# Placing TensorE's operands in SBUF at multiples of 2 KB, with the mixing outputs at staggered offsets

## The chip, the core and the metric

The kernel runs on one core of a Trainium2 chip. The metric is the time of one execution in device microseconds, as the median of several runs. All times below are microseconds unless they are marked ns. Offsets in SBUF are bytes from the start of a partition, the same on all 128 partitions.

## The reference

Two layers act on 256 positions of width 2048. Each layer is a mixing block and a feed-forward block, each with a residual and a layer norm behind it. The mixing block of layer 0 is a gated MLP plus a multiscale pool; that of layer 1 is a gated linear recurrence by chunks. All of them reduce to large products `h = x @ w`, and everything is float32.

```python
x:  [256, 2048]
layer 0:  h = x @ ev_w_in   # 2048 x 3072
          mix = concat(spatial_gating(h), multiscale_pool(h)) @ ev_w_out   # 2048 x 2048
layer 1:  h = x @ od_w_in   # 2048 x 8192
          mix = (rms_norm(hgrn2(h)) * sigmoid(g)) @ od_w_out               # 2048 x 2048
x = layer_norm(ALPHA * x + mix)
# in both layers
hc = conv3(x @ w_up)        # 2048 x 11264
x = layer_norm(ALPHA * x + (silu(hc[:, :5632]) * hc[:, 5632:]) @ w_down)   # 5632 x 2048
```

## The kernel before

**Products.** Weights come from HBM in tiles `w` of 128 x 4 x 512 floats (1 MB), through a ring of three. Each is split into two float32r tiles, `wh` (its rounded value, written by ScalarE at L144) and `wl` (the rest, written by VectorE at L147), in rings of three. The activations, transposed, are split in the same way into `xh` and `xl`. A product is then three matmuls for each of the four slices of 128 rows: `xh*wh`, `xh*wl`, `xl*wh` (L291, L359, L513). The activation slice of 128 columns (512 B a partition) is the stationary operand, which a weight load (PEld in the profile) puts into the array ahead of each matmul. The weight slice of 512 columns (2 KB a partition) is the moving one.

**Who uses which tiles.** `chunk` (L291) runs the mixing layers' input products on `xh`, `xl`, their output products on `yh`, `yl` (names `YT` in the code), and the first columns of a feed-forward block. `strassen` (L359) runs the rest of the up products on `xh`, `xl` and on combined tiles `sh`, `sl`; `down` and `last_down` (L513) run the down products on another `yh`, `yl`, which belong to the feed-forward block (`GT` in the code). So the name `y` stands for two sets of tiles: at L291 for the mixing outputs, at L513 for the feed-forward's.

**Order.** Each engine's instructions stand in the order in which the code issues them. Small work (transposes, gates, convolutions) is put between matmuls by `later` and `tick`.

**Where tiles lie.** Tile pools hand out SBUF in the order in which they are opened, one tile behind the other. The built program puts the operands of TensorE's large products here (offset, and what is left of it by 2048 and by 256):

| tiles | before | by 2048 | by 256 |
|---|---|---|---|
| `xh`, `xl` (8 tiles of 4 KB) | from 34464 | 1696 | 160 |
| `sh`, `sl` (2 of 8 KB) | from 67232 | 1696 | 160 |
| `wh`, `wl` (6 of 8 KB) | from 109600 | 1056 | 32 |
| mixing `yh`, `yl` (8 of 4 KB) | from 158752 | 1056 | 32 |
| feed-forward `yh`, `yl` (4 of 4 KB) | from 176544 | 416 | 160 |

A stationary slice begins a multiple of 512 B behind its tile's start, a moving slice a multiple of 2048 B.

Of the kernel before, what the change touches and what calls it, by code (L numbers as in the profile page):

```python
# [9 lines left out]
F32 = mybir.dt.float32  # L10
F32R = mybir.dt.float32r
# [7 lines left out]
P = 128  # L19
S = 256  # L20
D = 2048
DFF = 5632
NF = DFF // P
# [3 lines left out]
SKEW = 3  # L27
UNIT = ("P1", "s", "P2", "s", "P3", "o", "P7", "o", "P6", "o", "P5", "o", "P4", "s", "s")
BUFS = 3


class Weights:
# [78 lines left out]
    def room(self, kind):  # L111
# [6 lines left out]
        ring = self.ring.get(tag, [])  # L118
        n = 1 if kind else BUFS
        return len(ring) < n or ring[-n]["last"] < self.n_cast  # L120
# [46 lines left out]
def block_kernel(ctx: ExitStack, tc: tile.TileContext, a, out):  # L167
    nc = tc.nc
    V, A, G, T = nc.vector, nc.scalar, nc.gpsimd, nc.tensor

    const = ctx.enter_context(tc.tile_pool(name="const", bufs=1))
    resid = ctx.enter_context(tc.tile_pool(name="resid", bufs=1))
    acts = ctx.enter_context(tc.tile_pool(name="acts", bufs=1))
    gbp = ctx.enter_context(tc.tile_pool(name="gbp", bufs=1))
    small = ctx.enter_context(tc.tile_pool(name="small", bufs=2))
    raw = {0: ctx.enter_context(tc.tile_pool(name="raw", bufs=BUFS))}
    hl = ctx.enter_context(tc.tile_pool(name="hl", bufs=3))
    dram = ctx.enter_context(tc.tile_pool(name="dram", bufs=1, space=bass.MemoryType.DRAM))
# [32 lines left out]
    plan_ffn(1)  # L211


    cst = const.tile([P, 3, P], F32, name="cst")
    ident, tri, aft = (cst[:, i] for i in range(3))
    mhalf = const.tile([P, 4], F32, name="mhalf")
# [3 lines left out]
    def new_T(kind, g, pool=acts):  # L220
        h = pool.tile([P, 4, S], F32R, name=f"{kind}h{g}", tag=f"{kind}h{g}")
        l = pool.tile([P, 4, S], F32R, name=f"{kind}l{g}", tag=f"{kind}l{g}")
        return h, l

    def split(dst, src, hs, scale=None):

        h, l = dst[0][hs], dst[1][hs]
        if scale is None:
            A.activation(h, src, AF.Copy)
            V.tensor_tensor(out=l, in0=src, in1=h.bitcast(F32), op=ALU.subtract)  # L230
        else:
            A.activation(h, src, AF.Copy, scale=scale)
            V.scalar_tensor_tensor(out=l, in0=src, scalar=scale, in1=h.bitcast(F32),
                                   op0=ALU.mult, op1=ALU.subtract)

    XT = [new_T("x", g) for g in range(4)]
    with tc.tile_pool(name="xload", bufs=2) as xl:

# [25 lines left out]
    def later(n, fn):  # L264
        waiting.append([n, fn])
# [173 lines left out]
    def transpose(dst, src):  # L439
        T.transpose(dst, src, ident)  # L440
# [20 lines left out]
    def transpose_split(dst, src, t):  # L461

        pt = aux.tile([P, 4, P], F32, name="pt", tag="aux")
        for k in range(4):
            transpose(pt[:, k], src[:, k * P:(k + 1) * P])
        split(dst, pt, np.s_[:, :, t * P:(t + 1) * P])
# [8 lines left out]
    def out_proj(Ts_by_chunk, n, scale_first, g_ap=None, b_ap=None, order=None, final=False):  # L475

        last = g_ap is not None
        if last:
            gt, bt = load_gb(g_ap, b_ap)
            sts = [small.tile([P, 4, 6], F32, name=f"st{t}") for t in range(2)]  # L480
            new = [new_T("x", g) for g in range(4)] if not final else None
# [42 lines left out]
    def down(c, Ts, scale):  # L524

        w = W.take()
        for t in range(2):
            ps = aux.tile([P, 512], F32, name="pd", tag="aux")
            product(ps, w, Ts, t)
            tick(0.5)  # L530
            add_x(t, c, ps, scale)

    def last_down(Ts, g_ap, b_ap, final):

        gt, bt = load_gb(g_ap, b_ap)
        sts = [small.tile([P, 4, 6], F32, name=f"st{t}") for t in range(2)]
        new = [new_T("x", g) for g in range(4)] if not final else None
        pool_of = {}

# [62 lines left out]

    ymix = ExitStack()
    yp = ymix.enter_context(tc.tile_pool(name="ymix0", bufs=1))
    YT = [new_T("y", g, yp) for g in range(4)]
    with tc.tile_pool(name="work0", bufs=1) as wk:
        v_t = [wk.tile([P, 1024], F32, name=f"v{t}") for t in range(2)]
        b_t = [wk.tile([P, 1024], F32, name=f"xb{t}") for t in range(2)]
# [44 lines left out]
        def pool(gi):  # L653
# [13 lines left out]
            for d in range(2):  # L667
                kb = (gi % 2) * 2 + d
                split(YT[2 + gi // 2], py[:, d], np.s_[:, kb, :], scale=psc[:, gi * 2 + d:gi * 2 + d + 1])

        def after_u(c):
            def f(t, ps):
                u = wk.tile([P, 512], F32, name="u", bufs=2)
                A.activation(u, ps, AF.Gelu_apprx_tanh)
                V.tensor_tensor(out=u, in0=u, in1=v_t[t][:, c * 512:(c + 1) * 512], op=ALU.mult)
                later(1, lambda: transpose_split(YT[c], u, t))
            return f
# [14 lines left out]
        chunk(XT, 4, after_u(1))  # L692
        XT = out_proj([YT[g] for g in (2, 3, 0, 1)], 4, True, a["ln1_g"][0], a["ln1_b"][0])
    ymix.close()


    def ffn(l, XT, final):
        with ExitStack() as pools:
            wk = pools.enter_context(tc.tile_pool(name=f"workf{l}", bufs=1))
            raw[1] = pools.enter_context(tc.tile_pool(name=f"rawq{l}", bufs=1))  # L700
            W.open += 1
            cw = wk.tile([P, 4, 2 * NF], F32, name="cw")
            G.dma_start(cw, a["conv"][l].rearrange("p (j n) -> p j n", j=4))

            def h_tile(name="h", tag=None):
                return wk.tile([P, 512], F32, name=name, tag=tag or "h", bufs=1 if tag else 4)

            GT = {}

            def post(p, part, hs, hc):  # L710

                o = wk.tile([P, 4, S], F32, name="hc", tag="hc", bufs=2)
                hc[part] = o
                if part == 1:
                    GT[p] = tuple(wk.tile([P, 4, S], F32R, name=f"y{i}", tag=f"y{i}", bufs=2) for i in "hl")
                for kk in range(2):
                    pt = aux.tile([P, 2, S], F32, name="ph", tag="aux")
                    for k in range(2):
                        for tt in range(2):
                            fs = slice((2 * kk + k) * P, (2 * kk + k + 1) * P)  # L720
                            transpose(pt[:, k, tt * P:(tt + 1) * P], hs[tt][:, fs])
                    two = np.s_[:, 2 * kk:2 * kk + 2]
                    for k in range(2):
                        blk = part * NF + p * 4 + 2 * kk + k
                        ob = o[:, 2 * kk + k]
                        A.activation(ob, pt[:, k], AF.Identity, scale=cw[:, 2, blk:blk + 1],  # L726
                                     bias=cw[:, 3, blk:blk + 1])
                        for s, w in ((2, 0), (1, 1)):
                            V.scalar_tensor_tensor(  # L729
                                out=ob[:, s:S], in0=pt[:, k, 0:S - s], scalar=cw[:, w, blk:blk + 1],  # L730
                                in1=ob[:, s:S], op0=ALU.mult, op1=ALU.add)
                    if part == 0:
                        A.activation(o[two], o[two], AF.Silu)
                    else:
                        V.tensor_tensor(out=o[two], in0=o[two], in1=hc[0][two], op=ALU.mult)
                        split(GT[p], o[two], two)

            def ready(p):
                hc = {}
                return lambda part, hs: later(0.5 if part and p == 10 else 1, lambda: post(p, part, hs, hc))  # L740

            def conv(part, done):
                hs = [h_tile() for _ in range(2)]

                def f(t, ps):
                    A.activation(hs[t], ps, AF.Copy)
                    if t == 1:
                        done(part, hs)
                return f

            done = ready(0)
            chunk(XT, 4, conv(0, done), head=True)
            XS = combine(XT, lambda: wk.tile([P, 4, S], F32, name="cmb", tag="hc", bufs=2))
            chunk(XT, 4, conv(1, done))
            for p in range(1, 11):
                downs = [lambda c=c, p=p: down(c, GT[p - 1], p == 1) for c in range(4)]
                strassen(XT, XS, h_tile, ready(p), downs[:4 if p < 10 else 2])
            for fn in downs[2:]:
                fn()
            XT = last_down(GT[10], a["ln2_g"][l], a["ln2_b"][l], final)  # L760
            del raw[1]
        return XT

    XT = ffn(0, XT, False)


    yp = ymix.enter_context(tc.tile_pool(name="ymix1", bufs=1))
    YT = [new_T("y", g, yp) for g in range(4)]
    with tc.tile_pool(name="work1", bufs=1) as wk:
        lb = gbp.tile([P, D], F32, name="lb", tag="g")  # L770
        omlb = gbp.tile([P, D], F32, name="omlb", tag="b")
# [15 lines left out]
        def heads4(hg):  # L787
# [111 lines left out]
            def after_g(t, ps):  # L899
                g = wk.tile([P, 512], F32, name="gg", tag="tb", bufs=2)  # L900
                A.activation(g, ps, AF.Sigmoid)
                V.tensor_tensor(out=o_s[t], in0=o_s[t], in1=g, op=ALU.mult)
                later(1, lambda: transpose_split(YT[hg], o_s[t], t))

# [5 lines left out]
        for hg in range(4):  # L910
            heads4(hg)
        XT = out_proj(YT, 4, True, a["ln1_g"][1], a["ln1_b"][1])
    ymix.close()

    ffn(1, XT, True)


# [74 lines left out]
```

## Time and profile before

| | us |
|---|---|
| median of 3 runs (lowest to highest) | 2256.62 (2254.83 to 2259.21) |
| the profiled execution's own time | 2258.18 |
| span of its trace | 2256.5 |
| TensorE matmuls (PE) busy | 2215.6, 9971 instructions |
| weight loads (PEld) busy | 1803.7 |
| VectorE (DVE) busy | 1672.4 |
| ScalarE (ACT) busy | 1165.1 |
| GpSimd (POOL) busy | 103.4 |
| DMA | 466.98 MB, mean 207 GB/s |

Matmuls overlap in the profile: one takes some 0.39 from its start to its modelled end, while the next starts some 0.23 behind it. How fast TensorE works is therefore read from the distance between starts (called a step below), not from busy time.

### The profile page before, as it was taken

How to read it: one execution, taken by the hardware profiler on the slowest of the kernel's cores; microseconds unless marked ns; L12 is line 12 of the kernel's file. 1: busy time of each engine (PE TensorE's matmuls, PEld its weight loads, DVE VectorE, ACT ScalarE, POOL GpSimd, SP SyncE). 2: the span in 40 equal slices, each digit the busy share in tenths (PEclk: the TensorE clock that was granted, in tenths of full speed). 3: DMA queues.
4: the chain of work that ended last, by engine and by line, in shares of the span. 5: the costliest groups of instructions: out<-in, count | busy, mean ns of one | idle time of the engine just before them, and what ended most of it. 6: DMA issues, size and time to landing. Idle time of an engine off the chain costs nothing. (4 is left out here: it accounts for less than half of the span.)

```text
span 2256.5 us, 24752 instructions
## 1 busy us (share of the span) xinstructions
PE 2215.6 (98%) x9971; PEld 1803.7 (80%) x9971; DVE 1672.4 (74%) x1604; ACT 1165.1 (52%) x1088; POOL 103.4 (5%) x116
## 2 busy tenths in 40 slices
PE   9999999999999999979999999999999999999997
PEld 7888788888888888868888888878888888888885
DVE  5545878888888888876455555578788888888887
ACT  5443455555555555535354554336555555555552
POOL 1000200000000000020000000020000000000000
PEclk9999999999999999989999999999999999999999
DMA  8647456767766676535444454845777667677742
GB/s 316 261 161 277 159 179 218 230 224 242 218 213 220 214 235 224 187 126 193 158 167 173 167 210 168 279 153 168 226 241 242 202 211 221 216 232 243 239 149 116
DMA packets 68595, 466.98 MB, mean 207 GB/s; under 512 B 8080, under 2 KB 8736, under 8 KB 13312
## 3 DMA queue, kind: packets, MB, share of 16 engines
q1 hardware_dynamic: 60656, 411.56, 50.0%
q0 software_dynamic: 7824, 53.84, 11.5%
q8 instruction: 78, 1.28, 0.2%
q14 instruction: 37, 0.30, 0.0%
HBM read 421.32 MB, written 2.11 MB: 188 GB/s over the span
## 5 line engine op out<-in xcount | busy, mean ns | idle before, releaser
L147 DVE TENSOR_TENSOR wl<-w,wh 128x2048 fp32r<-128x2048 f32 (+1 forms) x450 | 1004.3, 2234 | 463.8 <-ACT wh L144 463.6
L144 ACT ACTIVATE wh<-w 128x2048 fp32r<-128x2048 f32 (+1 forms) x474 | 854.1, 1807 | 726.2 <-PE pd L513 260.5
L359 PE MATMUL ps<-wh,xh 128*128 128x512 f32 x880 | 350.5, 398 | 0.0
L359 PE MATMUL ps<-wh,xl 128*128 128x512 f32 x880 | 347.4, 395 | 0.0
L359 PE MATMUL ps<-wl,xh 128*128 128x512 f32 x880 | 347.0, 394 | 0.0
L291 PE MATMUL ps<-wh,xh 128*128 128x512 f32 x832 | 334.4, 403 | 1.2 <-ACT wh L144 1.2
L291 PE MATMUL ps<-wl,xh 128*128 128x512 f32 x832 | 330.1, 397 | 0.6 <-DVE wl L147 0.5
L291 PE MATMUL ps<-wh,xl 128*128 128x512 f32 x832 | 329.2, 396 | 0.0
L513 PE MATMUL pd<-wh,yh 128*128 128x512 f32 x664 | 263.0, 396 | 0.0
L513 PE MATMUL pd<-wl,yh 128*128 128x512 f32 x664 | 262.6, 395 | 0.0
L513 PE MATMUL pd<-wh,yl 128*128 128x512 f32 x664 | 261.9, 395 | 0.0
L359 PEld LDWEIGHTS ps<-wh,xl 128*128 128x128 f32 x880 | 165.7, 188 | 38.8
L359 PEld LDWEIGHTS ps<-wl,xh 128*128 128x128 f32 x880 | 165.9, 189 | 36.9
L359 PEld LDWEIGHTS ps<-wh,xh 128*128 128x128 f32 x880 | 165.8, 188 | 37.0
L291 PEld LDWEIGHTS ps<-wh,xh 128*128 128x128 f32 x832 | 157.7, 190 | 37.5 <-ACT wh L144 2.6
L291 PEld LDWEIGHTS ps<-wl,xh 128*128 128x128 f32 x832 | 157.7, 190 | 36.7 <-DVE wl L147 2.4
L291 PEld LDWEIGHTS ps<-wh,xl 128*128 128x128 f32 x832 | 157.3, 189 | 36.4
L513 PEld LDWEIGHTS pd<-wh,yl 128*128 128x128 f32 x664 | 125.4, 189 | 29.4
L513 PEld LDWEIGHTS pd<-wh,yh 128*128 128x128 f32 x664 | 125.5, 189 | 29.2
L513 PEld LDWEIGHTS pd<-wl,yh 128*128 128x128 f32 x664 | 125.4, 189 | 29.3
L729 DVE SCALAR_TENSOR_TENSOR hc<-ph,cw,hc 128x254 f32<-128x254 f32 (+1 forms) x352 | 145.7, 476 | 1.0 <-ACT hc L726 1.0
L359 PE MATMUL ps<-wh,sh 128*128 128x512 f32 x320 | 126.3, 395 | 0.5 <-ACT u L371 0.5
(191 smaller groups left out, 2284.3 us busy)
## 6 DMA issues: line engine op xcount, KB each, us to landing
w<-in_w_up SPq DMA_DIRECT2D x176, 1024.0 KB, 4.9
w<-in_w_down SPq DMA_DIRECT2D x88, 1024.0 KB, 4.9
w<-in_w_od_in SPq DMA_DIRECT2D x64, 1024.0 KB, 4.8
w<-w POOLq DMA_DIRECT2D x40, 1024.0 KB, 8.0
w<-in_w_ev_in SPq DMA_DIRECT2D x20, 1024.0 KB, 5.5
w<-in_w_ev_out SPq DMA_DIRECT2D x16, 1024.0 KB, 4.9
w<-in_w_od_out SPq DMA_DIRECT2D x16, 1024.0 KB, 5.8
w<-in_w_ev_in SPq DMA_DIRECT2D x16, 256.0 KB, 6.1
```

The lines of the kernel that those rows point to most:

```text
L144: self.nc.scalar.activation(h[:, sl], w[:, sl], AF.Copy)
L147: eng.tensor_tensor(out=l[:, sl], in0=w[:, sl], in1=h[:, sl].bitcast(F32), op=ALU.subtract)
L291: T.matmul(ps[t], s[:, k, ts], m[:, k], start=(gi == 0 and k == 0 and i == 0), stop=(gi == n - 1 and k == 3 and i == 2))
L359: T.matmul(bank_, x[:, k, ts], m[:, k], start=(id(bank_) not in started), stop=(end and k == 3 and i == 2), skip_group_check=True)
L513: T.matmul(ps, x[:, k, t * P:(t + 1) * P], m[:, k], start=(k == 0 and i == 0), stop=(k == 3 and i == 2))
L729: V.scalar_tensor_tensor(out=ob[:, s:S], in0=pt[:, k, 0:S - s], scalar=cw[:, w, blk:blk + 1], in1=ob[:, s:S], op0=ALU.mult, op1=ALU.add)
```

## The change

The pool `small` is opened ahead of the large pools instead of behind them, and a tile `edge` of 976 B fills up to 20480, so that all that follows, up to the weights' tiles, begins at multiples of 2048. The tile `cw` (the convolution's coefficients, 1408 B) gets a pool of its own behind the feed-forward's, so that it no longer stands ahead of their tiles. The mixing outputs, which would then also begin at multiples of 2048, are spread by pads of 32 to 64 B (once 224 B): a different offset for each of the eight tiles.

```diff
+EDGE = 244
+STAGGER = ((0, 32, 64, 96, 128, 160, 192, 256), (0, 224, 288, 320, 352, 384, 416, 448))
...
     const = ctx.enter_context(tc.tile_pool(name="const", bufs=1))
+    small = ctx.enter_context(tc.tile_pool(name="small", bufs=2))
+    edge = ctx.enter_context(tc.tile_pool(name="edge", bufs=1))
     resid = ctx.enter_context(tc.tile_pool(name="resid", bufs=1))
     acts = ctx.enter_context(tc.tile_pool(name="acts", bufs=1))
     gbp = ctx.enter_context(tc.tile_pool(name="gbp", bufs=1))
-    small = ctx.enter_context(tc.tile_pool(name="small", bufs=2))
...
+    edge.tile([P, EDGE], F32, name="edge")
...
+    def staggered(pool, at):
+        tiles, end = [], 0
+        for i in range(8):
+            if at[i] > end:
+                pool.tile([P, (at[i] - end) // 4], F32, name=f"pad{i}")
+                end = at[i]
+            tiles.append(pool.tile([P, 4, S], F32R, name=f"y{'hl'[i % 2]}{i // 2}"))
+        return [(tiles[2 * g], tiles[2 * g + 1]) for g in range(4)]
...
-    YT = [new_T("y", g, yp) for g in range(4)]
+    YT = staggered(yp, STAGGER[0])
...
-            cw = wk.tile([P, 4, 2 * NF], F32, name="cw")
+            cwp = pools.enter_context(tc.tile_pool(name=f"cw{l}", bufs=1))
+            cw = cwp.tile([P, 4, 2 * NF], F32, name="cw")
...
-    YT = [new_T("y", g, yp) for g in range(4)]
+    YT = staggered(yp, STAGGER[1])
```

In the changed program the places are these:

| tiles | by 2048 | by 256 |
|---|---|---|
| `xh`, `xl`, `sh`, `sl`, `wh`, `wl`, feed-forward `yh`, `yl` | 0 | 0 |
| mixing `yh0`, `yl0`, ... `yl3`, layer 0 | 0, 32, 64, 96, 128, 160, 192, 256 | 0, 32, 64, 96, 128, 160, 192, 0 |
| mixing `yh0`, `yl0`, ... `yl3`, layer 1 | 0, 224, 288, 320, 352, 384, 416, 448 | 0, 224, 32, 64, 96, 128, 160, 192 |

The order of the instructions is the same on PE, DVE, ACT and SP. On POOL two rows move. First, how POOL stands around the end of the output product of layer 0 before the change (`cw` the convolution's coefficients, `w_0<-w_2` the first accumulating DMA between weight tiles, `rs` a layer norm's scale, `wl` weight splits done by POOL):

```order
L655 DMA wp<-in_w_pool 128x2x256 x2
L75 DMA w_0_1787<-w_2_1791 128x2048
L448 TENSOR_TENSOR rs<-rs,mhalf 128x1
L147 TENSOR_TENSOR wl_1592<-w_40_1523,wh_1591 128x512 x4
L147 TENSOR_TENSOR wl_1604<-w_41_1559,wh_1603 128x512 x4
L703 DMA cw<-in_conv 128x352
L448 TENSOR_TENSOR rs<-rs,mhalf 128x1
```

And the same place on POOL with the change, with its own line numbers:

```order
L669 DMA wp<-in_w_pool 128x2x256 x2
L718 DMA cw<-in_conv 128x352
L77 DMA w_0_1801<-w_2_1805 128x2048
L462 TENSOR_TENSOR rs<-rs,mhalf 128x1
L149 TENSOR_TENSOR wl_1603<-w_40_1534,wh_1602 128x512 x4
L149 TENSOR_TENSOR wl_1615<-w_41_1570,wh_1614 128x512 x4
L462 TENSOR_TENSOR rs<-rs,mhalf 128x1
```

The load of `cw` is issued one place ahead of the accumulating DMA, since `cw` no longer lies where the mixing outputs lie. The same move is made in layer 1.

## Rows read from the trace of the kernel before

**Rows 1.** The page, parts 1 and 2: busy time, granted clock.

```profile
PE 2215.6 (98%) x9971; PEld 1803.7 (80%) x9971; DVE 1672.4 (74%) x1604; ACT 1165.1 (52%) x1088; POOL 103.4 (5%) x116
...
PEclk9999999999999999989999999999999999999999
```

**Rows 2.** PE's waits on others: us in total, times, longest.

```profile
PE pt L440 <- DVE x L459: 19.1, 9, 4.1
```

**Rows 3.** PE's groups by line and form: busy us, mean ns, idle before.

```profile
L359 PE MATMUL ps<-wh,xh 128*128 128x512 f32 x880 | 350.5, 398 | 0.0
...
L291 PE MATMUL ps<-wh,xh 128*128 128x512 f32 x832 | 334.4, 403 | 1.2 <-ACT wh L144 1.2
...
L513 PE MATMUL pd<-wh,yh 128*128 128x512 f32 x664 | 263.0, 396 | 0.0
...
L359 PE MATMUL ps<-wh,sh 128*128 128x512 f32 x320 | 126.3, 395 | 0.5 <-ACT u L371 0.5
...
L291 PE MATMUL ps<-wh,yh 128*128 128x512 f32 x256 | 100.4, 392 | 0.0
...
L513 PE MATMUL ps<-wh,yh 128*128 128x512 f32 x40 | 16.7, 418 | 5.0 <-ACT yh L229 5.0
```

**Rows 4.** Timeline of PE, mixing output products: start, us, engine, line, instruction.

```profile
166.46 0.40 PE L291 MATMUL ps<-wl,yh 128*128 128x512 f32 x1
...
243.53 0.39 PE L291 MATMUL ps<-wh,yl 128*128 128x512 f32 x1
...
1420.13 0.39 PE L291 MATMUL ps<-wl,yh 128*128 128x512 f32 x1
...
1497.22 0.39 PE L291 MATMUL ps<-wh,yl 128*128 128x512 f32 x1
```

**Rows 5.** Timeline of PE, an input product of layer 1 and feed-forward turns.

```profile
1117.14 0.39 PE L291 MATMUL ps<-wl,xh 128*128 128x512 f32 x1
...
1141.78 0.40 PE L291 MATMUL ps<-wh,xl 128*128 128x512 f32 x1
...
771.65 0.39 PE L359 MATMUL ps<-wl,xh 128*128 128x512 f32 x1
...
837.53 0.39 PE L359 MATMUL ps<-wl,xh 128*128 128x512 f32 x1
...
890.05 0.39 PE L359 MATMUL ps<-wh,xl 128*128 128x512 f32 x1
...
686.36 0.40 PE L359 MATMUL ps<-wh,xh 128*128 128x512 f32 x1
686.61 0.40 PE L359 MATMUL ps<-wl,xh 128*128 128x512 f32 x1
```

**Rows 6.** Windows: length; PE, PEld, DVE, ACT, POOL busy (instructions); clock; DMA share, GB/s.

```profile
166.46:243.54 77.08, 77.08 (x342) 63.81 (x340) 42.28 (x34) 25.93 (x17) 2.08 (x3) 1.00 0.72 257
837.53:890.06 52.53, 52.53 (x228) 42.59 (x227) 44.77 (x39) 27.17 (x21) 0.84 (x1) 1.00 0.80 255
1117.14:1141.79 24.65, 24.65 (x108) 19.98 (x107) 14.82 (x14) 13.69 (x13) 0.00 (x0) 1.00 0.54 190
```

**Rows 7.** ACT's waits in the feed-forward block of layer 0 (310 to 960).

```profile
ACT wh L144 <- PE pd L513: 125.8, 39, 3.7
```

**Rows 8.** Timeline and window of PE in a stretch at the lower clock.

```profile
992.80 0.63 PE L513 MATMUL pd<-wl,yh 128*128 128x512 f32 x1
...
994.50 0.62 PE L513 MATMUL pd<-wh,yl 128*128 128x512 f32 x1
...
992.60:994.80 2.20, 2.20 (x6) 0.50 0.00 0
```

**Rows 9.** Timeline of POOL in layer 0, and ACT's uses of `cw`.

```profile
184.65 0.93 POOL L75 DMA_DIRECT2D w<-w  x1 [62.81 <-DVE st L494]
...
256.02 0.60 POOL L703 DMA_DIRECT2D cw<-in_conv  x1 [0.21 <-issue]
...
L726 ACT ACTIVATE hc<-ph,cw x176: 543/555/572, 288.2 to 2216.4; 128x256 f32<-128x256 f32 x176
```

## The prediction

> **What bounds the kernel now.** I read the page first. TensorE's matmuls are busy for 98% of the span, at the full granted clock in all slices but one [rows 1]. Then the waits of PE: the largest of them, the transposes behind a layer norm, is 19.1 us in 9 times [rows 2]. So the time is the sum of TensorE's own steps, and the other engines wait for it: in the feed-forward block ScalarE waits 125.8 us for a matmul of L513 to give a weight buffer free [rows 7]. A change of the time has to come out of the step from one matmul's start to the next, which no view prints. I took it from the timeline, as first and last start of an unbroken run over the number of steps in it. The groups give the counts: three of each kind, so 3 x (880 + 320 + 832 + 664 + 40) = 8,208 large matmuls on `x`, `s` and the feed-forward's `y`, and 3 x 256 = 768 on the mixing outputs [rows 3].
>
> The two sets don't run at one pace. A mixing output product takes 341 matmuls from 166.46 to 243.53: 77.07 / 340 = 226.7 ns a step; in layer 1 the same 340 steps take 77.09, 226.7 ns again [rows 4]. (The window counts 342, one of which began before it [rows 6].) The input product from 1117.14 to 1141.78 has 107 matmuls: 24.64 / 106 = 232.4 ns; a feed-forward turn from 837.53 to 890.05 has 227: 52.52 / 226 = 232.4 ns [rows 5, 6]. The granted clock is 1.00 in all three stretches [rows 6], which is the 2.4 GHz level. So a step costs 5.7 ns more wherever the stationary tile is not a mixing output.
>
> What differs? Not the code: the input product and the output product are both written by `chunk`, at L291, with the same three matmuls for a slice and the same moving tiles `wh`, `wl`. Not the load: DMA moves 257 GB/s beside the output product, and 190 and 255 beside the other two; VectorE is busy for 42.28 of 77.08 beside the output product, 14.82 of 24.65 beside the input product and 44.77 of 52.53 in the feed-forward [rows 6]. The first two are near each other, and 25 points more of VectorE leave the longer step where it is. What is left is the place. Mixing outputs and weights begin at the same remainder, 1056 by 2048; `xh` and `sh` are 640 ahead of the weights and the feed-forward's `yh` 640 behind. Both are 128 off by 256, and slices move this by multiples of 512 only, so that each product has one relation throughout. That fits one longer step for both, and a shorter one at distance 0.
>
> **The change, part by part.**
>
> *Large tiles to multiples of 2 KB.* All of the 8,208 matmuls get the relation that the output products have now: stationary and moving tile at the same remainder. I take the 226.7 ns step for them. Counted over the trace, 7,952 of them are followed by another large matmul 220 to 245 ns later; the other 256 stand beside transposes, behind waits or at the lower clock, where a step is (994.50 - 992.80) / 4 = 425 ns [rows 8], and are taken to stay. 7,952 x 5.7 ns = **-45.3 us**. Bounds of this term by the same rows: 8,208 x 5.7 = 46.8 if the rest shrinks too; nothing if it isn't the place.
>
> *Do the others follow?* They have to be 2.5% faster in the same stretches. VectorE would go from 44.77 / 52.53 = 85% to 87% in a feed-forward turn [rows 6], and its casts are ahead, since ScalarE's half of them waits for PE's buffers [rows 7]; DMA goes from 255 GB/s at a share of 0.80 to some 261 at 0.82 [rows 6]. So nothing takes over. The stalls at the layer norms stay as they are [rows 2].
>
> *Mixing outputs staggered.* These 768 now run at 226.7 ns, at distance 0. With the change `yh` is stationary twice and `yl` once in every three; weighing the tiles so, 64 + 32 of 384 matmuls of layer 0 and 64 of 384 of layer 1 keep a multiple of 256, and 608 of 768 get another distance. Some 748 of the steps are unbroken, so 608 / 768 x 748 = 592 steps are at stake. The trace has no distance but 0 and 128 for these products. Below: nothing, if 128 alone costs more and the rest as little as 0. Above: all at the longest single step of the feed-forward, 686.61 - 686.36 = 0.25 in rounded starts (241 ns unrounded), 592 x 14.3 = 8.5 us. At 232.4 ns it is 592 x 5.7 = 3.4. I take half of that, **+1.7 us**, as some of the distances should be as good as 0 and some as bad as 128.
>
> *`cw` and `small`.* The order of instructions changes on POOL alone: `cw` is issued one place earlier, ahead of the DMA at 184.65, and no longer at 256.02; its first use is at 288.2 [rows 9]. It was not waited for before and lands earlier now: nothing. It takes its wait from the DMA that stood at 184.65, so the scale of the layer norm behind them is not held up longer than before. If that cover went, the price would be one landing in each layer, some 5 us each.
>
> *Transposes.* Their operands move against each other as well: some 600 short matmuls whose step is about 0.11. The same share of it, 5.7 / 232.4, would be 2.7 ns each, 1.6 us either way. I take nothing.
>
> The sum, on the profiled execution's own time: 2258.2 - 45.3 + 1.7 = 2214.6. That execution was 1.6 over the median of the runs shown, so as a median **2213.0 us**, 1.9% less.
>
> **A rule against it.** The step differs by 5.7 ns between runs of the same instructions at the same clock [rows 4 to 6]. The Trainium skill says the opposite of what I conclude from this: in "TensorE: Matmul & The Clock Gate", section "Step-by-step: what each phase is for", the streamed operand and the weight load have independent read ports, and "Loading the next tile's weights doesn't steal SBUF read bandwidth from the running matmul"; and "SBUF — State Buffer", section "Who interferes with whom", has TensorE never wait on anyone. By that rule the place of a tile is worth nothing and the sum is 2256.6. This trace doesn't agree with the strict form of it, since 226.7 and 232.4 ns stand side by side; but it doesn't show that the place is the reason, and so the rule stays as the first rival.
>
> **The rivals.**
>
> *No change (0.07).* The place is not the reason, and something that I don't see in the rows sets the pace of the two kinds of product: then the 8,208 keep 232.4 ns, the mixing products 226.7, and the time is 2256.6. For it: only two products have the shorter step, both the output products of mixing layers. Against it: the longer step is the same to 0.1 ns at L291 and at L359 with L513, under different loads.
>
> *Slower (0.04).* It is not the distance but the place itself that counts, and a start at 0, which no large operand has before, is worse than either remainder that the trace has (32 and 160 by 256). The place is every feed-forward and input step. At the longest single step of the feed-forward, 241 ns, for all: 7,952 x 8.6 = 68 us, 2325. It decides from 232.4 ns on; at 233 the time is 0.2% above before.
>
> *More than forecast (0.03).* Even the output products are not at the floor: at the lower clock a step is 425 ns [rows 8], and half of that is 213. If a start at a whole 2 KB takes away the rest too, 7,952 x 19 = 151 us more or less all come off: 2106. The Trainium skill's "Back-to-back issue gap" ("TensorE: Matmul & The Clock Gate") would put an undisturbed step of 512 columns at some 216 ns; an estimate by it is 7,952 x 16.4 = 130 us off, 2126. Against this case: 680 steps at distance 0 all keep to 226.7.
>
> *Part of it (0.03).* A start at 0 lies between the two: 229.5 ns, 7,952 x 2.9 = 23 us off, 2234.
>
> **How the numbers follow.** My forecast has 0.83. Its own range: 46.8 off and no stagger gives 2209.8; 45.3 off and 8.5 for the stagger gives 2219.8. With 2 us for the transposes either way and the half spread of the runs, 2.2, this is 2206 to 2224. I give 2205 to 2225; all rivals lie outside it, which leaves out 17 in 100. A measurement of this kernel tells about 0.2% from nothing, 4.5 us. Faster by more than that: forecast, part and more, 0.89. Within it: 0.07. Slower: 0.04.
>
> **What the profile of the changed kernel would show.** Right: a run of large matmuls in the input products and in the feed-forward steps by 226 to 227.5 ns; a turn of the feed-forward, 65.88 from 771.65 to 837.53 before [rows 5], takes 64.3 (276 matmuls x 5.7 ns = 1.6 less); PE's waits for VectorE stay near 19 us and no wait for `wh` or `wl` appears in the feed-forward. The stagger: 77.1 for 340 steps of a mixing output product grows to between 77.1 and 81, and steps change when `chunk` goes on to the next group. Wrong: input and feed-forward steps that stay at 232 (the first rival) or rise; a step below 226; or steps at 226.7 with new gaps in front of matmuls, which would mean that the casts or the weight loads don't follow.

## The result, and the profile after

The changed kernel takes 2220.46 us (median of 4 runs, 2219.09 to 2221.51), the kernel before 2257.91 beside it (4 runs). The ratio is 0.9836, 95% interval 0.9819 to 0.9853: 1.6% faster. The profiled execution took 2219.09, its span 2217.4; against the one shown before that is 39.1 us less.

The page of the changed kernel, parts 1 and 2, to be read beside [rows 1]:

```profile
PE 2175.4 (98%) x9971; PEld 1798.1 (81%) x9971; DVE 1670.8 (75%) x1604; ACT 1161.9 (52%) x1088; POOL 102.8 (5%) x116
...
PEclk9999999999999999989999999999999999999998
```

The busy shares are the same within one point, and the clock in all slices but the last; VectorE and ScalarE have lost 1.6 and 3.2 us of busy time, TensorE 40.2. So TensorE still sets the time, and it got through the same 9971 instructions sooner. The timeline of PE shows where. Changed lines: L305 is L291 of before, L373 is L359, L527 is L513. First the input product and the feed-forward turn that answer to [rows 5]:

```profile
1097.30 0.40 PE L305 MATMUL ps<-wl,xh 128*128 128x512 f32 x1
...
1121.33 0.39 PE L305 MATMUL ps<-wh,xl 128*128 128x512 f32 x1
...
759.42 0.40 PE L373 MATMUL ps<-wl,xh 128*128 128x512 f32 x1
...
823.76 0.40 PE L373 MATMUL ps<-wl,xh 128*128 128x512 f32 x1
...
875.00 0.39 PE L373 MATMUL ps<-wh,xl 128*128 128x512 f32 x1
```

The same 106 steps now take 24.03, 226.7 ns each instead of 232.4. The 226 steps from 823.76 to 875.00 take 51.24, 226.7 ns instead of 232.4. A whole turn, 759.42 to 823.76, takes 64.34 instead of 65.88. The mixing output products, which answer to [rows 4], went the other way:

```profile
164.23 0.40 PE L305 MATMUL ps<-wl,yh 128*128 128x512 f32 x1
...
243.14 0.40 PE L305 MATMUL ps<-wh,yl 128*128 128x512 f32 x1
...
1395.04 0.39 PE L305 MATMUL ps<-wl,yh 128*128 128x512 f32 x1
...
1473.81 0.40 PE L305 MATMUL ps<-wh,yl 128*128 128x512 f32 x1
```

340 steps take 78.91 and 78.77 instead of 77.07 and 77.09: 232.1 and 231.7 ns. The windows over three of these stretches, beside [rows 6] (PE, PEld, DVE, ACT, POOL busy, clock, DMA share, GB/s), show that the load beside TensorE is what it was:

```profile
164.23:243.15 78.92, 78.92 (x342) 63.85 (x340) 42.61 (x34) 25.95 (x17) 2.65 (x4) 1.00 0.71 253
823.76:875.01 51.25, 51.25 (x228) 42.42 (x227) 44.66 (x39) 27.14 (x21) 0.85 (x1) 1.00 0.82 262
1097.30:1121.34 24.04, 24.04 (x108) 19.90 (x107) 14.70 (x14) 13.70 (x13) 0.00 (x0) 1.00 0.54 192
```

The waits of PE (us, times, longest) have hardly moved, as [rows 2] and the idle times of [rows 3] (5.0 at L513, 1.2 for `wh` at L291) say beside these lines; the waits for `wh` fall in the first 100 us, in the input product of layer 0:

```profile
PE pt L454 <- DVE x L473: 18.3, 9, 4.3
PE ps L527 <- ACT yh L243: 5.0, 2, 2.5
PE ps L305 <- ACT wh L146: 2.3, 2, 1.3
```

### The profile page after: what moved, and what is told of

Read it like the earlier page. It is cut to its first block, busy times and chain, and to the rows that moved or that the text cites. A ratio compares the mean times of both kernels' runs of the same rounds, so it can differ in the third digit from the quotient of the medians.

```text
span 2217.4 us, 24753 instructions
## 1 busy us (share of the span) xinstructions
PE 2175.4 (98%) x9971; PEld 1798.1 (81%) x9971; DVE 1670.8 (75%) x1604; ACT 1161.9 (52%) x1088; POOL 102.8 (5%) x116
## 5 line engine op out<-in xcount | busy, mean ns | idle before, releaser
L373 PE MATMUL ps<-wh,xh 128*128 128x512 f32 x880 | 345.8, 393 | 0.0
L373 PE MATMUL ps<-wh,xl 128*128 128x512 f32 x880 | 342.6, 389 | 0.0
L373 PE MATMUL ps<-wl,xh 128*128 128x512 f32 x880 | 342.6, 389 | 0.0
L305 PE MATMUL ps<-wh,xh 128*128 128x512 f32 x832 | 330.3, 398 | 2.3 <-ACT wh L146 2.3
L305 PE MATMUL ps<-wl,xh 128*128 128x512 f32 x832 | 325.8, 392 | 0.3 <-DVE wl L149 0.3
L305 PE MATMUL ps<-wh,xl 128*128 128x512 f32 x832 | 325.0, 391 | 0.0
L527 PE MATMUL pd<-wh,yh 128*128 128x512 f32 x664 | 259.1, 390 | 0.0
L527 PE MATMUL pd<-wl,yh 128*128 128x512 f32 x664 | 258.8, 390 | 0.0
L527 PE MATMUL pd<-wh,yl 128*128 128x512 f32 x664 | 258.4, 390 | 0.0
L373 PEld LDWEIGHTS ps<-wh,xl 128*128 128x128 f32 x880 | 165.2, 188 | 34.4
L373 PEld LDWEIGHTS ps<-wh,xh 128*128 128x128 f32 x880 | 165.3, 188 | 33.0
L373 PEld LDWEIGHTS ps<-wl,xh 128*128 128x128 f32 x880 | 165.3, 188 | 32.9
L305 PEld LDWEIGHTS ps<-wh,xh 128*128 128x128 f32 x832 | 156.9, 189 | 34.9 <-ACT wh L146 3.2
L305 PEld LDWEIGHTS ps<-wl,xh 128*128 128x128 f32 x832 | 156.9, 189 | 32.9 <-DVE wl L149 2.2
L305 PEld LDWEIGHTS ps<-wh,xl 128*128 128x128 f32 x832 | 156.6, 188 | 33.0
L527 PEld LDWEIGHTS pd<-wh,yl 128*128 128x128 f32 x664 | 124.9, 188 | 26.4 <-DVE yl L244 0.4
L527 PEld LDWEIGHTS pd<-wh,yh 128*128 128x128 f32 x664 | 125.0, 188 | 25.9
L527 PEld LDWEIGHTS pd<-wl,yh 128*128 128x128 f32 x664 | 124.9, 188 | 25.8
L373 PE MATMUL ps<-wh,sh 128*128 128x512 f32 x320 | 124.7, 390 | 0.5 <-ACT u L385 0.5
```

Of the source, the lines that this page charges most:

```text
L305: T.matmul(ps[t], s[:, k, ts], m[:, k], start=(gi == 0 and k == 0 and i == 0), stop=(gi == n - 1 and k == 3 and i == 2))
L373: T.matmul(bank_, x[:, k, ts], m[:, k], start=(id(bank_) not in started), stop=(end and k == 3 and i == 2), skip_group_check=True)
L527: T.matmul(ps, x[:, k, t * P:(t + 1) * P], m[:, k], start=(k == 0 and i == 0), stop=(k == 3 and i == 2))
```

## The experiments

Each kernel is named by what it changes. The times are medians beside runs of the kernel before on the same chip; steps are means over a trace's unbroken steps (220 to 245 ns), and where the text gives one without rows, it is counted over all of them. Every kernel below computes the whole reference.

**The changed kernel without the stagger.** Is it the stagger that lengthened the mixing products?

```diff
-STAGGER = ((0, 32, 64, 96, 128, 160, 192, 256), (0, 224, 288, 320, 352, 384, 416, 448))
+STAGGER = ((0,) * 8, (0,) * 8)
```

> The changed kernel without the stagger: the eight mixing outputs begin at multiples of 2048 too. Distance theory (a step is short when the stationary and the moving tile begin at the same remainder by 512): the steps of the two mixing output products go from 231.9 ns back to 226.7, 750 x 5.2 = 3.9 us less than the changed kernel, about 2216.5 as a median; the input and feed-forward steps stay at 226.7 to 227.5. If the longer mixing steps after the change came from something else in the new layout, they stay at 231.9 and the time at 2220.5.

Measured: 2216.8 (5 runs; ratio 0.9821, interval 0.9808 to 0.9834). The timeline of this kernel, the mixing output product of layer 0:

```profile
163.50 0.40 PE L305 MATMUL ps<-wl,yh 128*128 128x512 f32 x1
...
240.57 0.39 PE L305 MATMUL ps<-wh,yl 128*128 128x512 f32 x1
```

340 steps in 77.07, 226.7 ns: the value of before is back. Over the trace, 748 mixing steps average 226.8 ns where the changed kernel's 750 average 231.9, which is 3.8 us where 3.9 were expected; the medians differ by 3.7. The two were timed against runs of before on two occasions and their intervals overlap, so it is the steps that carry this, not the ratio.

**The kernel before with two pads of 640 B.** Does a start at 2 KB matter, or the distance alone?

```diff
+    edge = ctx.enter_context(tc.tile_pool(name="edge", bufs=1))
     raw = {0: ctx.enter_context(tc.tile_pool(name="raw", bufs=BUFS))}
...
+    edge.tile([P, 160], F32, name="edge")
...
             cw = wk.tile([P, 4, 2 * NF], F32, name="cw")
+            wk.tile([P, 160], F32, name="edge")
```

> The kernel before with two pads of 640 B alone: every large operand begins at 1696 by 2048 and nothing at a multiple of 2 KB. Distance theory: all large matmuls step by 226.7 ns, and the time is that of the layout at multiples of 2 KB without the stagger, about 2216.5. Alignment theory (a start at a whole 2 KB, or at another whole power of two above 32, is what helps): the steps stay at 232.4 and the time at 2257.9.

Measured: 2216.88 (4 runs; ratio 0.9822, interval 0.9808 to 0.9835), the same as without the stagger, with every large operand at 1696 by 2048. The timeline, a feed-forward turn, lines as before but two further down:

```profile
822.28 0.40 PE L361 MATMUL ps<-wl,xh 128*128 128x512 f32 x1
...
873.52 0.40 PE L361 MATMUL ps<-wh,xl 128*128 128x512 f32 x1
```

226 steps in 51.24, 226.7 ns. The alignment theory is out: nothing here begins at a multiple of more than 32 B.

**A gap ahead of the weights: 256, 480, 192 and 32 B.** On the layout without the stagger, a gap between the activations and the weights sets the distance of `x` and `s` to the weights and leaves both `y` at distance 0, since they lie behind the weights and move with them. What does each distance cost? The lines below are for 256 B; the other gaps have `[P, 120]`, `[P, 48]` and `[P, 8]`.

```diff
+    gap = ctx.enter_context(tc.tile_pool(name="gap", bufs=1))
     raw = {0: ctx.enter_context(tc.tile_pool(name="raw", bufs=BUFS))}
...
+    gap.tile([P, 64], F32, name="gap")
```

256 B:

> The layout of e1_even with a gap of 256 B ahead of the weight tiles and of all that follows: xh, xl, sh, sl at 0 by 2048, weights, mixing and feed-forward y at 256. Distance theory: the 5,864 steps on x and s go from 226.7 to about 231.3 (the changed kernel's 32 steps at 256), the y products stay at 226.7; 27 us over e1_even, about 2243. Alignment or stationary's own place: x and s stay at 226.7, their starts are untouched, and the y products change instead (about 2,100 + 750 steps). A distance that counts by 256 (my assumption in the prediction): no change against e1_even.

480 B:

> As e3_gap256 with a gap of 480 B: the stationary x and s lie 32 B ahead by 512. Distance theory with a price that depends on the distance: the changed kernel has its longest steps there, 236.5 ns, so 5,864 x 9.8 = 57 us over e1_even, about 2274, slower than the kernel before. If every distance but 0 costs the same 5 ns, about 2246. Stationary's own place: as e1_even, about 2216.5.

192 B:

> As e3_gap256 with a gap of 192 B: x and s lie 64 B ahead of the weights by 256. If only distance 0 by 256 is free: 5,864 steps x 5 to 6 ns, 29 to 37 us over e1_even, about 2246 to 2253. If a distance of 64 is free as well (a period of 64), as e1_even, 2216.5.

32 B:

> As e3_gap256 with a gap of 32 B: x and s lie 224 B ahead of the weights by 256, or 32 behind. If the price is the same on both sides of 0: as e4_gap480, 2253. If a stationary tile that lies behind the moving one is free or dearer, the steps on x and s leave 233 ns for 227 or for 235 (the changed kernel's steps at 224): 2217 or 2265.

| gap | `x`, `s` ahead of weights, by 256 | median (runs) | ratio, 95% interval | steps on `x` and `s` |
|---|---|---|---|---|
| 0 | 0 | 2216.8 (5) | 0.9821, 0.9808 to 0.9834 | 226.7 to 227.4 |
| 256 | 0 | 2216.36 (4) | 0.9818, 0.9805 to 0.9831 | 226.7 to 227.4 |
| 480 | 32 | 2253.27 (10) | 0.9982, 0.9973 to 0.9991 | 233.0 to 233.3 |
| 192 | 64 | 2254.91 (10) | 0.9983, 0.9973 to 0.9992 | 233.2 to 233.3 |
| 32 | 224 | 2252.32 (8) | 0.9973, 0.9963 to 0.9984 | 232.8 to 233.3 |

With the gap of 256 B the timeline reads

```profile
820.86 0.40 PE L375 MATMUL ps<-wl,xh 128*128 128x512 f32 x1
...
872.10 0.39 PE L375 MATMUL ps<-wh,xl 128*128 128x512 f32 x1
```

51.24 for 226 steps. I had expected a longer step here, because the changed kernel's trace has 32 steps at distance 256 that average 231.3 (a step counted by the tile that is loaded during it). Those stand among steps at distance 192 (`yl3` at 256 beside `yh3` at 192), and in that trace most steps at distance 0 are longer where tiles at other distances take turns with them. With the distance held for a whole product, 256 is as good as 0, and the distance counts by 256, as the prediction had it. With the gap of 480 B, the input product and, from 166.38, the mixing output product:

```profile
1316.15 0.39 PE L307 MATMUL ps<-wl,xh 128*128 128x512 f32 x1
...
1340.88 0.40 PE L307 MATMUL ps<-wh,xl 128*128 128x512 f32 x1
...
166.38 0.40 PE L307 MATMUL ps<-wl,yh 128*128 128x512 f32 x1
...
243.45 0.39 PE L307 MATMUL ps<-wh,yl 128*128 128x512 f32 x1
```

24.73 / 106 = 233.3 ns on `x`, 77.07 / 340 = 226.7 on `y`, side by side in one kernel. The same input product with the gaps of 192 B and 32 B:

```profile
1113.06 0.39 PE L307 MATMUL ps<-wl,xh 128*128 128x512 f32 x1
...
1137.80 0.40 PE L307 MATMUL ps<-wh,xl 128*128 128x512 f32 x1
...
1113.73 0.40 PE L307 MATMUL ps<-wl,xh 128*128 128x512 f32 x1
...
1138.47 0.39 PE L307 MATMUL ps<-wh,xl 128*128 128x512 f32 x1
```

Both take 24.74 for the 106 steps, 233.4 ns. The activations lie at multiples of 2 KB in all five rows of the table, so it isn't the stationary tile's own place; and the `y` products, whose weights moved by 480, 192 or 32 B, kept their step, so it isn't the moving tile's place either. (The mixing products average 226.8 to 226.9 ns in all of them. The feed-forward's `y` average 227.1 to 227.6 at these three gaps, against 226.8: in the runs of 24 steps between runs on `x` and `s`, some of the first seven steps or the last are longer, and those between keep to 226.6 to 226.8.) The distances 32, 64 and 224 cost 6.1 to 6.6 ns a step and 128, in the kernel before, 5.7: any distance but 0 costs about the same, where I had expected 236.5 at 32 from the changed kernel's mixed steps.

**Two pads of 128 B in the kernel before.** The smallest edit that the rule by 256 allows: the pads of 640 B cut to `[P, 32]`.

> The kernel before with two pads of 128 B: one ahead of the weight tiles, one ahead of the feed-forward's tiles, so that all large operands begin at 160 by 256, at 1696, 1184 and 672 by 2048. Distance by 256: all large steps at 226.7 and 2216.8 as e1_even and e2_pads. Distance by 512 or more: the feed-forward's y keeps distance 512 and is free as well, but a period of 1024 or 2048 would leave x, s and y at 232.4 and the time at 2257.

Measured: 2217.18 (4 runs; ratio 0.9816, interval 0.9801 to 0.983). A feed-forward turn:

```profile
822.09 0.39 PE L361 MATMUL ps<-wl,xh 128*128 128x512 f32 x1
...
873.34 0.39 PE L361 MATMUL ps<-wh,xl 128*128 128x512 f32 x1
```

51.25 / 226 = 226.8 ns, though `x`, the weights and the feed-forward's `y` begin at 1696, 1184 and 672 by 2048. So 256 B of pads (128 B in two places) give the kernel before all that the changed layout gives. The median is 3.3 us below the changed kernel's, which fits the stagger's 3.8; the two were timed on two occasions and their intervals overlap, so the 3.3 by itself is not shown.

**One displaced tile: `xl` alone.** Which read meets which? Here the four `xl` tiles lie 128 B off, and the rest at distance 0.

```diff
+    gap = ctx.enter_context(tc.tile_pool(name="gap", bufs=1))
+    actl = ctx.enter_context(tc.tile_pool(name="actl", bufs=1))
+    gap2 = ctx.enter_context(tc.tile_pool(name="gap2", bufs=1))
...
+    gap.tile([P, 32], F32, name="gap")
+    gap2.tile([P, 32], F32, name="gap2")
...
-    def new_T(kind, g, pool=acts):
-        h = pool.tile([P, 4, S], F32R, name=f"{kind}h{g}", tag=f"{kind}h{g}")
-        l = pool.tile([P, 4, S], F32R, name=f"{kind}l{g}", tag=f"{kind}l{g}")
+    def new_T(kind, g):
+        h = acts.tile([P, 4, S], F32R, name=f"{kind}h{g}", tag=f"{kind}h{g}")
+        l = actl.tile([P, 4, S], F32R, name=f"{kind}l{g}", tag=f"{kind}l{g}")
```

> The layout of e1_even with the four xl tiles alone 128 B off by 256; xh, sh, sl, both y and the weights keep distance 0. Theory A (the weight load of the next matmul collides with the moving read of the present one): of the three steps of a slice, the one that begins at wl*xh, during which xl is loaded, gets longer; the one that begins at wh*xl, during which xh is loaded, stays at 226.7. Theory B (a matmul is longer when its own stationary tile is off its moving tile): the step that begins at wh*xl gets longer. Some 1,640 steps of each kind on x: at 5.7 ns 9 us over e1_even, about 2226; if a delayed load pushes the step behind it too, up to 19 us, 2235. s and y stay at 226.7 in both.

Measured: 2234.94 (4 runs; ratio 0.9893, interval 0.9878 to 0.9908). On `x` the step at `wh*xh` averages 227.3 ns, at `wl*xh` 232.4, at `wh*xl` 233.7; `s` and both `y` stay at 226.7 to 226.8. In the timeline, an input product:

```profile
1104.08 0.39 PE L310 MATMUL ps<-wh,xh 128*128 128x512 f32 x1
...
1108.25 0.39 PE L310 MATMUL ps<-wh,xh 128*128 128x512 f32 x1
```

18 steps take 4.17, 695 ns for three where 3 x 226.7 are 680. So both steps that touch `xl`, the one beside its load and the one that uses it, are longer, by 5 to 7 ns. Neither A nor B alone says so; A with a push on the next step does, and gave 2235.

**One displaced tile: `wl` alone.** Carry or own tile?

```diff
-        l = self.hl.tile([P, 4, 512], F32R, name=f"wl{i}", tag="wl")
+        l = self.hll.tile([P, 4, 512], F32R, name=f"wl{i}", tag="wl")
...
+    gap = ctx.enter_context(tc.tile_pool(name="gap", bufs=1))
+    hll = ctx.enter_context(tc.tile_pool(name="hll", bufs=3))
+    gap2 = ctx.enter_context(tc.tile_pool(name="gap2", bufs=1))
...
+    gap.tile([P, 32], F32, name="gap")
+    gap2.tile([P, 32], F32, name="gap2")
```

> The layout of e1_even with the three wl tiles alone 128 B off by 256; all stationary tiles keep distance 0 to wh. In e5_xl128 one displaced tile lengthened two steps of three, that at wl*x (232.4), during which xl is loaded, and that at wh*xl (233.7). Carry theory: only a load beside a moving tile at another distance collides, and the step behind it pays for the delay. Then here again the steps at wl*xh (the load of xl beside wl) and at wh*xl are longer, on x, s and both y: 2,900 x (5.8 + 7.0) = 37 us over e1_even, about 2254. Own-tile theory: a matmul collides with the load of its own stationary tile as well as with that of the next. Then the two collisions of wl fall on the step at wl*xh and on the start of the same matmul, so that wh*xl stays at 226.7 to 227.3: 2,900 x 5.8 to 12.8 = 17 to 37 us, 2234 to 2254.

Measured: 2265.12 (6 runs; ratio 1.0033, interval 1.002 to 1.0045), slower than the kernel before. The timeline in a feed-forward turn:

```profile
843.64 0.40 PE L378 MATMUL ps<-wh,xh 128*128 128x512 f32 x1
843.87 0.40 PE L378 MATMUL ps<-wl,xh 128*128 128x512 f32 x1
844.11 0.39 PE L378 MATMUL ps<-wh,xl 128*128 128x512 f32 x1
...
847.84 0.40 PE L378 MATMUL ps<-wh,xh 128*128 128x512 f32 x1
```

From 843.64 to 847.84 stand 18 steps: 233.3 ns each. In the down products the three kinds average 235.4 at `wh*yh`, 234.0 at `wl*yh` and 229.9 at `wh*yl`: all three are longer, and the longest is the one at which neither the moving tile nor the tile being loaded is displaced. The carry theory expected that one at 226.7, and the own-tile theory expected `wh*yl` there; both fall. The order is not the same everywhere: on `x` in `chunk` (L310) the three average 232.4, 231.3 and 231.7. That this kernel is slower than the one before comes in good part from the mixing outputs, which had distance 0 before and lose it to `wl` here: 748 steps go from 226.8 to 232.1 ns, 4.0 us of the 6.7 between the medians. Which accesses are behind it stays open.

## Why the prediction was right

*The place, not the load.* Right, and now shown: the large tiles step by 226.7 to 227.5 ns whether they all begin at 0 or at 1696 by 2048, or at 1696, 1184 and 672, and a gap of 480 B brings the longer step back for the tiles that it displaces, while the others keep theirs but for steps next to a run on the displaced ones. The rival without change is out by the kernel with two pads of 128 B, which changes nothing but places. The other three rivals fall with the 226.7 ns of the changed kernel, which is neither above 232.4 nor at 213 nor halfway, at 229.5. The Trainium skill, in "TensorE: Matmul & The Clock Gate", "Step-by-step: what each phase is for", has the weight load leave the running matmul its read bandwidth. This case doesn't agree with it as far as it would make the place worth nothing: a matmul's step depends on where the loaded tile lies, 226.7 against 232.4 to 233.3 ns. That it is bandwidth that is lost is not shown.

*Distance by 256.* Right; the prediction assumed it from two distances, 0 and 128, and the gap of 256 B shows it, as do the pads of 128 B, with `x` 512 B off the weights by 2048.

*-45.3 for the large tiles.* Right to 2 us. In the profiled executions the unbroken steps on `x`, `s` and the feed-forward's `y` were 45.3 us over 226.7 ns a step, and are 2.2 over it now: 43.1 less. The remaining 2.2 are mostly the input products' steps, which average 227.5 and not 226.7.

*+1.7 for the stagger.* Too low: 750 steps went from 226.8 to 231.9 ns, 3.8 us. The term was halved because some of the distances were taken to be as good as 0. None is: by the tile that is loaded during the step, the distances other than 0 average 230.5 to 236.5 ns. The bound at 232.4 ns, 3.4, was nearer, and the steps at distance 0 that stand among others (226.7 to 231.3 ns) are mostly longer too. The range held because its upper end allowed 8.5 for this term.

*The others follow.* Right: no wait of PE for a cast appeared in the feed-forward, and DMA went from 255 to 262 GB/s in the turn. VectorE's work, nearly the same, now fills 87% of it (44.66 / 51.25).

*`cw` one place earlier.* Right as far as the waits show, worth nothing. POOL's timeline in layer 0 shows it issued at 164.74, the accumulating DMA behind it at 181.59 (184.65 before [rows 9]), and the layer norm's scale waiting for VectorE as ever:

```profile
164.74 0.55 POOL L718 DMA_DIRECT2D cw<-in_conv  x1 [44.62 <-PE pt L454]
181.59 0.91 POOL L77 DMA_DIRECT2D w<-w  x1 [16.31 <-DMA w<-in_w_up]
241.49 0.93 POOL L462 TENSOR_TENSOR rs<-rs,mhalf 128x1 f32<-128x1 f32 x1 [58.98 <-DVE rs L459]
```

The sum: all unbroken large steps of the trace took 2017.7 us before (8,700 of them) and 1980.7 now (8,710); all the rest of the span 238.8 and 236.7. That the rest fell by 2.1 says nothing of its own: ten more steps, 2.3 us, count as unbroken now. On the profiled execution I forecast 43.6 less and 39.1 were measured; 2.1 of the difference are the stagger and 2.2 the large tiles. The median of 2220.5 is 7.5 over the forecast of 2213.0, since the runs of the changed kernel also lie 1.4 over its profiled execution, while I took the median to lie 1.6 under it.

## What to carry to other kernels

Where TensorE is busy without a gap, compare the step between starts of equal matmuls in different parts of the program: two paces for the same instruction at the same clock are a loss that no busy share and no wait shows. Here they came from the distance in SBUF between the stationary and the moving tile, and two pads of 128 B were enough, one ahead of the weights' tiles and one ahead of the feed-forward's; what counted is that both operands, and all moving tiles that take turns, have the same remainder by 256, not that either is aligned. All runs here are of float32r tiles with 128 columns stationary and 512 moving; other types and shapes were not tried. Moving one tile of such a set alone can cost more than it gains: the kernel with `wl` displaced is slower than the kernel before.

## What the hardware showed that I had not expected

- Any distance by 256 other than 0 that was held through a product (32, 64, 128, 224) costs 5.7 to 6.6 ns of a step of 226.7; there is no gentle slope near 0. Distances finer than 32 B were not tried, and 96, 160 and 192 were not held through a product.
- In the changed kernel's mixing products, where tiles at different distances take turns, the steps average 230.5 to 236.5 ns by the distance of the tile loaded, and some of those at distance 0 between them rise to 231.
- With one of two moving tiles 128 B off, all three steps of a slice are longer. In the down products their sum (235.4, 234.0, 229.9 ns) is more than if the stationary tiles are 128 B off both moving ones (3 x 232.4); in `chunk`, on `x`, it is less (232.4, 231.3, 231.7).
- At distance 0 a step is 226.7 ns and not 213, half of the 425 at the lower clock [rows 8]. What the other 13 ns are stays open.
